# A two-layer transformer kernel on one core: first-stage loads laid out by tile, constant matmuls, token tiles in pairs

## The chip, the core and the metric

The kernel runs on one core of a Trainium2 chip. A core has five engines with queues of their own: PE (TensorE: matmuls and transposes through the array), DVE (VectorE), ACT (ScalarE), POOL (GpSimd) and SP (SyncE, which here issues nearly all DMAs). Results of PE go to PSUM, which has eight banks; everything else lies in SBUF or in HBM. The metric is the device time of one execution in microseconds, and the median of several executions is compared.

## The reference, cut to what matters

Two layers run over 1024 tokens of width 1024, with 256 context tokens beside them. Layer 0 is attention with 16 query heads and 4 key/value heads; layer 1 is neighbourhood attention. Each layer starts with a norm that is modulated by a conditioning vector, and ends with a gated output projection.

```
silu_c = jax.nn.silu(c); silu_cc = jax.nn.silu(c_ctx)
for i in range(DEPTH):
    mod_x = (silu_c @ w_mod[i] + b_mod[i])[:, None, :]
    mod_c = silu_cc @ w_mod[i] + b_mod[i]
    sh_x, sc_x, g_x = jnp.split(mod_x, 3, axis=-1)
    sh_c, sc_c, g_c = jnp.split(mod_c, 3, axis=-1)
    hx = rms_norm(x, norm_g[i]) * (1.0 + sc_x) + sh_x
    hc = rms_norm(ctx, norm_g[i]) * (1.0 + sc_c) + sh_c
    if i % N_MIXERS == 0:
        yx, yc = gqa_axial_mixer(hx, hc, a_w_in[ia], ..., a_w_out[ia], cos, sin, not last)
    else:
        yx, yc = neighbourhood_mixer(hx, hc, b_w_in[ib], b_rpb[ib], b_w_out[ib], not last)
    x = x + g_x * yx
    if not last:
        ctx = ctx + g_c * yc
return rms_norm(x, final_norm_g)

# gqa_axial_mixer, its beginning
px = hx @ w_in                      # columns: q 1024, k 256, v 256, z 1024
q = apply_axial_rope(rms_norm(q, q_g), cos, sin)
k = apply_axial_rope(rms_norm(k, k_g), cos, sin)
pkv = hc @ w_in[:, A_WIDTH:A_WIDTH + 2 * A_KV_WIDTH]
```

## The kernel before

Tokens are cut into ten tiles of 128: tiles 0 to 7 are x, tiles 8 and 9 the context. The width of 1024 is cut into eight steps, kt = 0 to 7. Matmuls that need more than f16 are done three times, with both factors split into a high and a low f16 part (hi·hi, hi·lo, lo·hi).

**First stage.** For each kt, `mod_cols` loads two f32 tiles `wm` (512 KiB each, in two DMAs of 256 KiB whose contiguous pieces are 512 B) of the layer's modulation weights. It multiplies them with the conditioning vector (`pm`), copies the row (`mrow`), turns it into columns (`pmc`) and forms the scale and shift, `acol` and `scol`. The pool has seven `wm` buffers, so the loads can run three and a half steps ahead. `ln_pre` loads a token tile (`xstage`, 512 KiB) and normalises it in place. `h_kt(t0, n, kt)` transposes one kt block of n token tiles on PE (`pl`), applies scale and shift on ACT (`tf`), and splits into a high part (a cast) and a low part (a subtract), both on DVE. `load_w` loads 256 KiB of weights (`wskv`), scales them to a high part on ACT and takes the low part on DVE. `kv_mm` does three matmuls of 512 columns per tile and kt into the tile's k/v bank (`pkv`). `kv_post` takes v out, normalises and rotates k (`norm_rope_split`: `sq`, `qss`, a power on POOL `qrs`, `t1k`, `t2k`, a multiply with `qrs`, the split `q16k`) and transposes it (`pkt`).

The first part of the stage is the loop over kt for tiles 0 to 3, which keeps four banks open. The second part transposes tiles 4 to 7, four at a time, and the context tiles, and runs tiles 4 to 9 through two banks at a time. Then layer 0's attention follows: per pair of heads a projection (`pa`, with weights `wsa`), scores, softmax and values, on all engines. Output projection (`poa`), layer 1's projections (`pb`, `pvz`, weights `wsb`), its attention (`bsn`, `bpv`) and the last projection (`pob`, weights `wsob`) end the program.

**What sets the order.** The code is written out once in a rough order (the functions `timeline` and `items` give each piece of work a place). Then `Planner` builds a graph of all instructions with a table of costs, lists them for each engine, goes back from the end to due times, and lists them again five times; the best list becomes the order on each engine. So each change in code or costs may move instructions anywhere.

What the changed lines call is below, with the profile's line numbers.

Of the kernel before, what the change touches and what calls it, by code (L numbers as in the profile page):

```python
# [40 lines left out]
PFB, PHB, PTB = 5, 5, 8  # L41


class Planner:
# [42 lines left out]
    def cost(self, x, rd, wr):  # L87
# [6 lines left out]
        if e == "PE":  # L94
            f32 = ins[0].dtype == mybir.dt.float32
            cols = self.elems(outs[0])
            passes = (2 if x.is_transpose else 4) if f32 else 1
# [59 lines left out]
    def graph(self):  # L157
# [60 lines left out]
        for i, x in enumerate(self.node):  # L218
# [4 lines left out]
            before[e] = i  # L223

# [33 lines left out]
    def schedule(self, key=None, margin=0.0, scale=None):  # L258
# [62 lines left out]
        while count < N:  # L321
# [86 lines left out]
            for j in succ[i]:  # L408
                rdy[j] = max(rdy[j], fin + self.SEM[self.eng[j]] + margin if self.eng[j] != e or e != "PE" else 0.0)
# [6 lines left out]
    def deadlines(self, margin):  # L416
# [14 lines left out]
        for i in sorted(range(N), key=lambda i: -start[i]):  # L431
            e, d = self.eng[i], done[i] - start[i]
            for j in self.succ[i]:
                due[i] = min(due[i], due[j] - (0.0 if self.eng[j] == e == "PE" else d + self.SEM[self.eng[j]] + margin))
# [47 lines left out]
def trunk_kernel(ctx, tc, x, cx, cc, norm_g, ng_row, b_cols, sel_c, w_mod, b_mod, a_w_in, a_qg, a_kg, a_w_out,  # L482
                 b_w_in, rpb, b_w_out, fin_g, cos_t, sin_t, mask_q, out):
# [29 lines left out]

    cct = main.tile([P, 2 * KT], F32, name="cct")
# [186 lines left out]
    def norm_rope_split(pool, sqs, psv, alt, nt, nh, t0, gc, gs, gplain, nm):  # L701
# [26 lines left out]
        if alt is None:  # L728
            V.tensor_tensor(t1, t1, rb, op=ALU.mult)
# [17 lines left out]

    def a_src(kt0, nk, ncol):

        starts = ncol  # L750
        wd = 512 // (nk * len(starts))
        step = starts[1] - starts[0] if len(starts) > 1 else wd

        def f(st):
            for j in range(nk):
                a = a_w_in[(kt0 + j) * P:(kt0 + j + 1) * P, starts[0]:starts[0] + 1]
                src = bass.AP(a.tensor, a.offset, [[2560, P], [step, len(starts)], [1, wd]])
                ins = DM.dma_start(st[:, j * (512 // nk):(j + 1) * (512 // nk)].rearrange("p (r c) -> p r c", c=wd),
                                   src)
            return ins  # L760
        return f
# [27 lines left out]
    def h_kt(t0, n, kt):  # L789
# [8 lines left out]
        V.tensor_copy(hi[:, kt, c], tv)  # L798
# [20 lines left out]
    def ps_kv(t):  # L819
        tag = "st" if t % 4 < 2 else "pv"  # L820
# [6 lines left out]
    for kt in range(KT):  # L827
        load_w(wkv, a_src(kt, 1, [1024, 1280]), kt, 1, 512, f"kv{kt}")
        if kt + 1 < KT:
            mod_cols(kt + 1, wmp)  # L830
        if kt >= 4:
            ln_pre(kt)
# [3 lines left out]
        for t in range(4):  # L836
            kv_mm(banks[t], t, kt)
    for t in range(8, 10):
# [358 lines left out]
    def load_wout(src, nm):  # L1197
        ws = []
        wout[nm] = ws
        for hf in range(2):  # L1200
# [325 lines left out]
    items.append((load_wout(b_w_out, "b"), 6.9, 7.2, 1600))  # L1526
# [112 lines left out]
```

## Time and profile before

| what | value |
|---|---|
| three runs | 1380.61, 1385.62, 3514.45 us; median 1385.62 |
| the profiled execution | 1390.31 us, its span 1388.5 us |
| PE busy | 1331.3 us, 96% of the span |
| DVE, ACT, POOL busy | 73%, 66%, 46% |
| DMA | 198.22 MB, 143 GB/s on average, the queues 65% busy |
| first k/v matmul of tiles 0 to 3 | 23.7 us |
| first matmul of tiles 4 to 9's part (after the last of tiles 0 to 3) | 64.2 us |
| first projection of layer 0's queries (`pa`) | 108.6 us |

The page's busy times are for one execution. A line of the chain or of the waits names an engine, a line of the kernel and the tile. A wait is put down to what came last. In the views by stretch the busy time of each engine stands with its number of instructions, and the granted clock is that of PE.

### The profile page before, as it was taken

The page shows a single profiled execution, that of the slowest core. Times are in us where ns is not written, and L with a number is a line of the kernel's source. Part 1 is how long each engine was busy: PE and PEld are TensorE (multiplying, and loading weights), DVE is VectorE, ACT ScalarE, POOL GpSimd, SP SyncE. Part 2 cuts the span into 40 slices and gives each one's busy share as a digit, 9 for nine tenths or more (in the row PEclk, how much of TensorE's full clock was granted, in tenths as well). Part 3 has the DMA queues.
Part 4 walks back from the last instruction along what each step waited for, and adds up shares of the span by engine and source line. Part 5 has one row for each costly group of instructions (what it writes and reads, how often), then busy time and mean ns, then how long its engine had stood idle before and what let it go on. Part 6 is the DMA issues. An engine that isn't in the chain of part 4 may idle for free.

```text
span 1388.5 us, 34562 instructions
## 1 busy us (share of the span) xinstructions
PE 1331.3 (96%) x13082; PEld 921.5 (66%) x13082; DVE 1008.4 (73%) x2674; ACT 911.8 (66%) x2178; POOL 641.3 (46%) x811
## 2 busy tenths in 40 slices
PE   5799999999999999999999999999999999999897
PEld 3457777777767677676554476867767686867543
DVE  3597887879878888889347746677776768687733
ACT  2553687878787787687733427677777767787811
POOL 2222677777677768677954301212122222322332
PEclk9999999999999999999999999999999999999999
DMA  9744458778688878674328734576766756587922
GB/s 266 241 118 114 89 122 161 141 154 171 125 162 158 159 149 162 130 194 122 112 86 214 185 91 114 103 150 126 128 136 119 150 106 150 94 173 136 215 84 99
DMA packets 478927, 198.22 MB, mean 143 GB/s; under 512 B 383328, under 2 KB 455968, under 8 KB 478760
## 3 DMA queue, kind: packets, MB, share of 16 engines
q1 hardware_dynamic: 478184, 195.99, 65.2%
q8 instruction: 102, 1.67, 0.5%
q14 instruction: 65, 0.53, 0.1%
q10 hardware_dynamic: 576, 0.03, 0.0%
HBM read 90.51 MB, written 15.22 MB: 76 GB/s over the span
## 4 chain that ended last, share of the span: by engine, by line
PE 71%; DVE 12%; DMA 6%; ACT 5%; issue 3%; POOL 2%; SPq 0%; DVEq 0%; POOLq 0%; ACTq 0%
PE pvz L1378 11%; PE pa L928 11%; PE pb L1345 9%; PE poa L1258 7%; PE pob L1550 5%; PE pkv L803 3%; PE st L1165 2%; PE st L1166 2%; DVE mxp L959 2%; PE bpv L1458 2%; PE pm L958 2%; DMA qpt<-qpp 2%; DMA xstage<-in_x 2%; PE qpv L1086 1%; PE pv L1034 1%
## 5 line engine op out<-in xcount | busy, mean ns | idle before, releaser
L1027 POOL TENSOR_TENSOR pl<-pf,ph 128x256 f16<-128x256 f32 x340 | 234.4, 715 | 58.7 <-ACT pf L1152 43.0
L1027 POOL TENSOR_TENSOR bph<-bpf,bph 128x256 f16<-128x256 f32 (+1 forms) x128 | 98.2, 778 | 312.7 <-ACT bpf L1449 248.0
L928 PE MATMUL pa<-wa,x 128*128 128x256 f16 x1536 | 212.4, 272 | 0.0
L1345 PE MATMUL pb<-hb_hi,wb 128*128 128x512 f16 (+1 forms) x640 | 192.6, 358 | 0.5 <-DVE bk L1364 0.4
L1378 PE MATMUL pvz<-wb,hb_hi 128*128 128x256 f16 x1024 | 176.2, 273 | 3.7 <-DVE bk L1364 3.2
L1150 ACT ACTIVATE ph<-st 128x512 f16<-128x512 f32 x200 | 119.1, 604 | 69.3 <-PE st L1166 56.5
L928 PEld LDWEIGHTS <-x 128*128 128x128 f16 x1536 | 143.0, 97 | 32.2 <-issue 1.1
L1345 PEld LDWEIGHTS <-wb 128*128 128x128 f16 x960 | 92.6, 98 | 73.7 <-issue 1.5
L1378 PE MATMUL pvz<-wb,hb_lo 128*128 128x256 f16 x512 | 139.6, 273 | 0.0
L959 DVE TENSOR_REDUCE mxp<-pm 128x1 f32<-128x512 f32 x160 | 107.8, 683 | 20.5 <-PE pm L958 19.6
L1152 ACT ACTIVATE pf<-st 128x512 f32<-128x512 f32 x200 | 118.7, 608 | 1.8 <-POOL pl L1027 1.8
L1378 PEld LDWEIGHTS <-hb_hi 128*128 128x128 f16 x1024 | 97.1, 98 | 26.9 <-DVE bk L1364 5.8
L1345 PE MATMUL pb<-hb_lo,wb 128*128 128x512 f16 (+1 forms) x320 | 114.5, 358 | 0.0
L1027 POOL TENSOR_TENSOR qpp<-qpf,qpp 128x512 f16<-128x512 f32 x84 | 97.3, 1178 | 35.9 <-ACT qpf L1109 31.0
L1033 PE MATMUL pv<-v,ph 128*128 128x65 f16 x800 | 105.5, 193 | 0.2 <-DVE og L1015 0.2
L1034 PE MATMUL pv<-v,ph 128*128 128x64 f16 x800 | 105.0, 195 | 0.0
L1035 PE MATMUL pv<-v,pl 128*128 128x65 f16 x800 | 102.7, 192 | 1.7 <-DVE pl L1024 1.4
L1447 ACT ACTIVATE bph<-bpf,bnx 128x384 f16<-128x384 f32 (+1 forms) x128 | 69.7, 584 | 36.8 <-DVE bnx L1439 36.5
L1429 DVE CUSTOM_DVE_ANT_0 bpf<-bsn,tb 128x384 f32<-128x384 f32 x96 | 53.0, 552 | 55.5 <-PE bsn L1410 53.4
L1550 PE MATMUL pob<-wob,ob 128*128 128x512 f16 x384 | 87.3, 379 | 3.3 <-DVE bmx L1429 1.1
L1033 PEld LDWEIGHTS <-ph 128*128 128x128 f16 x800 | 75.8, 97 | 20.9 <-DVE og L1015 0.4
L1035 PEld LDWEIGHTS <-pl 128*128 128x128 f16 x800 | 76.1, 99 | 14.4 <-POOL pl L1027 3.5
(268 smaller groups left out, 3802.5 us busy)
## 6 DMA issues: line engine op xcount, KB each, us to landing
wg<-in_w_mod SPq DMA_DIRECT2D x64, 256.0 KB
wsb<-in_b_w_in SPq DMA_DIRECT2D x64, 256.0 KB
wm<-in_w_mod SPq DMA_DIRECT2D x32, 256.0 KB
wsa<-in_a_w_in SPq DMA_DIRECT2D x64, 128.0 KB
xstage<-in_x SPq DMA_DIRECT2D x8, 512.0 KB
wsoa<-in_a_w_out SPq DMA_DIRECT2D x16, 256.0 KB
x<-in_x SPq DMA_DIRECT2D x8, 512.0 KB
x_d<-x SPq DMA_DIRECT2D x8, 512.0 KB
```

The source lines that it names most:

```text
L928: T.matmul(ps[:, :, i, :], hA(a, kt, t), wt[w][:, kt, :], start=n == 0, stop=n == 3 * KT - 1)
L959: V.tensor_reduce(mxs[i][:, t, ch:ch + 1], pm, axis=AX.X, op=ALU.max)
L1027: G.tensor_tensor(lo[:, c], p32[:, c], hi[:, c], op=ALU.subtract)
L1033: T.matmul(pv[:, t, :], hi[:, c], v[:, 0:65], start=first and t == 0, stop=False)
L1034: T.matmul(pv[:, t, 0:HD], hi[:, c], v[:, 65:129], start=False, stop=False)
L1035: T.matmul(pv[:, t, :], lo[:, c], v[:, 0:65], start=False, stop=last and t == n - 1)
L1150: S.activation(ph, st, AF.Exp)
L1152: S.activation(p32, st, AF.Exp)
L1258: T.matmul(ps, lhs(a, kt), w[b][:, kt, :], start=n == 0, stop=n == 3 * KT - 1)
L1345: T.matmul(ps[:, 0:n].rearrange("p (t q) -> p t q", q=P), wt[a][:, kt, which * P:(which + 1) * P], hb[b][:, c0 // P:(c0 + n) // P, kt], st ...
L1378: T.matmul(ps[:, :, j, :], hb[a][:, t, kt], wt[w][:, kt, 256:512], start=m == 0, stop=m == 3 * KT - 1)
L1550: T.matmul(ps, ob[kt][:, t // 4, a, c], wout["b"][hf][b][:, kt, :], start=n == 0, stop=n == 3 * KT - 1)
```

## The change

Layouts on the host: the modulation weights of layer 0 become `w_mod0`, in which one `wm` tile is one piece of 4 KiB per partition, loaded by one DMA of 512 KiB. The k/v columns are a tensor of their own (`a_kv`). The q/z columns of a pair (`a_qz`) and layer 1's input weights (`b_in`) lie so that each load reads pieces of 2 KiB and not of 512 B.

In the program: 101 matmuls of a constant tile (`warm`, 256 columns) that depend on nothing else and whose result nobody reads. A soft rule for the planner (`BEHIND`): the loads of x tiles 4 to 7 are issued after that of `wskv7`. Tiles 4 to 7 are transposed in two pairs, not four at a time. For all tiles but 0 to 3 the cast to the high part moves from DVE to POOL, and for k tiles the multiply with `qrs` and the subtract of the split move from DVE to POOL. Half 0 of the last projection's weights gets an earlier place in the rough order.

```
+BEHIND = [(f"xstage{t}", "wskv7") for t in range(4, 8)]
...
+        for late, early in BEHIND:
+            self.soft.add((writer[early], writer[late]))
+            self.pred[writer[late]].add(writer[early])
...
+    wone = main.tile([P, 2 * P], F16, name="wone")
+    V.memset(wone, 1.0)
+    warm = ps_mx("warm")
+    def warm_up(n):
+        for _ in range(n):
+            T.matmul(warm[:, 0:2 * P], wone[:, 0:P], wone, start=True, stop=True)
+    warm_up(1)
...
-            for r in range(2):
-                a = w_mod[0, 4 * j * P:4 * j * P + P, r * D + kt * P:r * D + kt * P + 1]
-                DM.dma_start(wm[:, :, r, :], bass.AP(a.tensor, a.offset, [[3 * D, P], [P * 3 * D, 4], [1, P]]))
+            DM.dma_start(wm.rearrange("p a b c -> p (a b c)"), w_mod0[kt, j])
...
-        if alt is None:
-            V.tensor_tensor(t1, t1, rb, op=ALU.mult)
+        off = alt is None
+        if off:
+            G.tensor_tensor(t1, t1, rb, op=ALU.mult)
...
-        V.tensor_tensor(q16[:, :, 1, :], alt, q16[:, :, 0, :], op=ALU.subtract)
+        (G if off else V).tensor_tensor(q16[:, :, 1, :], alt, q16[:, :, 0, :], op=ALU.subtract)
...
-        V.tensor_copy(hi[:, kt, c], tv)
+        (G if t0 else V).tensor_copy(hi[:, kt, c], tv)
...
-        load_w(wkv, a_src(kt, 1, [1024, 1280]), kt, 1, 512, f"kv{kt}")
+        load_w(wkv, lambda st, kt=kt: DM.dma_start(st, a_kv[kt]), kt, 1, 512, f"kv{kt}")
...
-        if kt >= 4:
-            ln_pre(kt)
+        if kt >= 6:
+            ln_pre(2 * kt - 8)
+            ln_pre(2 * kt - 7)
...
+    warm_up(100)
...
-        h_kt(4, 4, kt)
+        h_kt(4, 2, kt)
         if kt % 2:
             kv_post(banks[kt // 2], kt // 2)
+    for kt in range(KT):
+        h_kt(6, 2, kt)
...
-            load_w(wa[u], a_src(2 * j, 2, [u * P, 1536 + u * P]), 2 * j, 2, 256, f"a{u}{j}")
+            load_w(wa[u], lambda st, j=j: DM.dma_start(st, a_qz[u, :, 512 * j:512 * j + 512]), 2 * j, 2, 256, f"a{u}{j}")
...
-                a = b_w_in[kt * P:(kt + 1) * P, u * P:u * P + 1]
-                DM.dma_start(st.rearrange("p (r c) -> p r c", c=P),
-                             bass.AP(a.tensor, a.offset, [[4 * D, P], [D, 4], [1, P]]))
+                DM.dma_start(st, b_in[u, :, kt * 512:kt * 512 + 512])
...
-    items.append((load_wout(b_w_out, "b"), 6.9, 7.2, 1600))
+    items.append((load_wout(b_w_out, "b", (0,)), 6.05, 6.9, 800))
+    items.append((load_wout(b_w_out, "b", (1,)), 7.0, 7.3, 800))
```

**How the order moves.** Three places, with the numbers of the tiles; the last figure of a name only tells buffers apart.

SP at the very start, before: `wm00` and `wm01` are the two halves of step 0's modulation weights, each loaded by two DMAs, `xstage0` is x tile 0.

```order
L551 DMA wm00_149<-in_w_mod 128x4x128
L551 DMA wm01_152<-in_w_mod 128x4x128
L781 DMA xstage0_107<-in_x 128x1024
L551 DMA wm10_215<-in_w_mod 128x4x128
L551 DMA wm11_218<-in_w_mod 128x4x128
L781 DMA xstage1_108<-in_x 128x1024
L781 DMA xstage2_109<-in_x 128x1024
```

The second DMAs of these four, `xstage3`, and the first DMAs of steps 2 and 3 follow before `wskv0`, the first k/v weights: twelve `wm` DMAs and four x tiles in all. SP at the same place now:

```order
L795 DMA xstage0_111<-in_x 128x1024
L795 DMA xstage1_112<-in_x 128x1024
L795 DMA xstage2_113<-in_x 128x1024
L795 DMA xstage3_114<-in_x 128x1024
L579 DMA wm00_153<-in_w_mod0 128x1024
L579 DMA wm01_155<-in_w_mod0 128x1024
L579 DMA wm10_217<-in_w_mod0 128x1024
L579 DMA wm11_219<-in_w_mod0 128x1024
L842 DMA wskv0_213<-in_a_kv 128x512
```

The four x tiles are issued first, then steps 0 and 1 of `wm`, each in two DMAs and not in four, and `wskv0`.

SP in the later half of the first part, before: x tiles 4 to 7 among the k/v weights of steps 4 to 7.

```order
L781 DMA xstage4_111<-in_x 128x1024
L758 DMA wskv4_399<-in_a_w_in 128x512
L781 DMA xstage5_112<-in_x 128x1024
L551 DMA wm60_459<-in_w_mod 128x4x128
L551 DMA wm61_462<-in_w_mod 128x4x128
L781 DMA xstage6_113<-in_x 128x1024
L758 DMA wskv5_455<-in_a_w_in 128x512
```

And now, from `wskv4` on:

```order
L842 DMA wskv4_393<-in_a_kv 128x512
L579 DMA wm60_442<-in_w_mod0 128x1024
L579 DMA wm61_444<-in_w_mod0 128x1024
L579 DMA wm70_487<-in_w_mod0 128x1024
L579 DMA wm71_489<-in_w_mod0 128x1024
L842 DMA wskv5_438<-in_a_kv 128x512
L842 DMA wskv6_483<-in_a_kv 128x512
L842 DMA wskv7_555<-in_a_kv 128x512
L795 DMA xstage4_115<-in_x 128x1024
L795 DMA xstage5_116<-in_x 128x1024
L781 DMA ct_151<-in_cos_t 128x512
```

The x tiles stand behind all weights of the first part; `ct` (a rope table), `gk`, `sn`, tiles 6 and 7 and the context tiles follow.

POOL at the beginning of the second part, before: the four rope tables and two norms, then only the powers of the k tiles (`qrsk`).

```order
L774 TENSOR_TENSOR gck_139<-ct_147,gk_132 128x512
L775 TENSOR_TENSOR gsk_140<-sn_148,gk_132 128x512
L609 TENSOR_TENSOR rs_ln_617<-ms_ln_615,mhalf_75 128x1
L609 TENSOR_TENSOR rs_ln_627<-ms_ln_625,mhalf_75 128x1
L774 TENSOR_TENSOR gcq_129<-ct_147,gq_131 128x512
L775 TENSOR_TENSOR gsq_130<-sn_148,gq_131 128x512
L711 TENSOR_TENSOR qrsk0_657<-qssk0_655,mhalf_75 128x4
```

And now, from the first cast (`x10` is the high part of x tiles 4 to 7, `tf40` the scaled block of kt 0 of the pair 4, 5):

```order
L812 CAST x10_109<-tf40_725 128x256
L812 CAST x10_109<-tf41_732 128x256
L739 TENSOR_TENSOR qrsk0_741<-qssk0_739,mhalf_75 128x4
L812 CAST x10_109<-tf42_763 128x256
L758 TENSOR_TENSOR t1k0_743<-t1k0_743,qrsk0_741 128x256
L812 CAST x10_109<-tf43_770 128x256
L739 TENSOR_TENSOR qrsk1_779<-qssk1_777,mhalf_75 128x4
L762 TENSOR_TENSOR q16k0_749<-t1k0_743,q16k0_749 128x4x64
```

Casts, powers, multiplies and splits alternate on POOL; 24 casts stand there up to the last that a k/v matmul of the context needs, with eight powers and fifteen multiplies and subtracts among them, and the tables `gcq` and `gsq`.

On PE the 101 constant matmuls stand ahead of the first `pkv`: 70 at the very start, then 11, 8, 4 and 8 between the first transposes and the first `pm` and `pmc`; the second `pm`, a step of transposes and the second `pmc` come after them, ahead of the first `pkv`. The eight loads of half 0 of `wsob` stand between the same transposes of layer 1 as before.

More of the change, by code (lines that the diff above doesn't have):

```diff
@@ L96, in cost @@
             cols = self.elems(outs[0])
+            if outs[0].bass_ap.tensor.name.startswith("warm"):
+                return 130.0, 170.0
             passes = (2 if x.is_transpose else 4) if f32 else 1
@@ L223, in graph @@
             before[e] = i
+        self.soft = set()
+        writer = {}
+        for i, x in enumerate(self.node):
+            if type(x).__name__ == "InstDMACopy" and x.outs and hasattr(x.outs[0], "bass_ap"):
+                writer.setdefault(x.outs[0].bass_ap.tensor.name.rsplit("_", 1)[0], i)
+        for late, early in BEHIND:
+            self.soft.add((writer[early], writer[late]))
+            self.pred[writer[late]].add(writer[early])
         self.glued = set()
@@ L481, in trunk_kernel @@
 @with_exitstack
-def trunk_kernel(ctx, tc, x, cx, cc, norm_g, ng_row, b_cols, sel_c, w_mod, b_mod, a_w_in, a_qg, a_kg, a_w_out,
-                 b_w_in, rpb, b_w_out, fin_g, cos_t, sin_t, mask_q, out):
+def trunk_kernel(ctx, tc, x, cx, cc, norm_g, ng_row, b_cols, sel_c, w_mod, w_mod0, b_mod, a_qz, a_kv, a_qg, a_kg, a_w_out,
+                 b_in, rpb, b_w_out, fin_g, cos_t, sin_t, mask_q, out):
     nc = tc.nc
@@ L746, in trunk_kernel @@
     sqk = sq_tiles(lp)
[L748 to L761, printed above, removed]
     ct = lp.tile([P, NX, HD], F32, name="ct")
@@ L1195, in trunk_kernel, with load_wout @@
     wout = {}
[L1197 to L1200, printed above, removed]
+    def load_wout(src, nm, halves=(0, 1)):
+        ws = wout.setdefault(nm, [])
+        for hf in halves:
             w = x_pair(hf, f"wo{nm}{hf}")
@@ L1600 @@
     rp = np.pad(i["b_rpb"][0].transpose(0, 2, 1), ((0, 0), (0, 0), (8, 8)))
+    aw = i["a_w_in"][0]
     arrs = {
@@ L1614 @@
         "a_w_out": i["a_w_out"][0],
-        "b_w_in": i["b_w_in"][0],
+        "b_in": i["b_w_in"][0].reshape(KT, P, 4, KT, P).transpose(3, 1, 0, 2, 4).reshape(KT, P, 4 * D),
         "rpb": rp,
```

15 lines of the change are left out of this document (12 added, 3 removed).

## The prediction

> **What bounds the kernel now.** I read the page first, then busy time by stretch, cut where PE changes its work, then the list of PE's waits, then the order of time in the first 110 us. Span 1388.5 us; the profiled execution took 1390.31 us, and the median of the three runs shown is 1385.62 us. The page's part 1:
>
> ```profile
> PE 1331.3 (96%) x13082; PEld 921.5 (66%) x13082; DVE 1008.4 (73%) x2674; ACT 911.8 (66%) x2178; POOL 641.3 (46%) x811
> ```
>
> PE is idle for only 57 us, so the question is where those are. Busy time by stretch (after the limits and the length come busy us and count of PE, PEld, DVE, ACT, POOL, then granted clock, DMA share, GB/s):
>
> ```profile
> core 0: us, PE busy (x) PEld busy (x) DVE busy (x) ACT busy (x) POOL busy (x), PEclk, DMA share, GB/s
> 0.00:23.70 23.70, 10.03 (x56) 5.76 (x57) 7.74 (x25) 8.17 (x13) 7.76 (x15) 1.00 0.98 279
> 23.70:64.20 40.50, 37.00 (x241) 17.91 (x239) 20.43 (x51) 15.26 (x26) 4.90 (x8) 0.96 0.82 254
> 64.20:108.60 44.40, 40.24 (x218) 21.62 (x217) 41.28 (x106) 24.41 (x56) 15.23 (x14) 0.92 0.51 121
> 108.60:240.00 131.40, 128.23 (x1460) 101.45 (x1458) 107.36 (x284) 87.89 (x187) 80.90 (x103) 1.00 0.58 124
> 240.00:660.00 420.00, 406.10 (x5169) 304.62 (x5168) 352.74 (x949) 327.97 (x671) 306.28 (x387) 0.99 0.74 152
> ...
> 1200.00:1310.00 110.00, 104.57 (x998) 74.81 (x997) 87.68 (x259) 89.39 (x270) 34.64 (x45) 1.00 0.84 160
> ```
>
> The first stage is the first three rows: 23.7 us up to the first k/v matmul, 40.5 us in which the eight kt steps of tiles 0 to 3 run (the "first part"), 44.4 us for tiles 4 to 9 (the "second part"). PE idles 13.7 + 3.5 + 4.2 = 21.4 us there, and in parts of it runs at a lower clock. From 108.6 to 660 us it idles 3.2 + 13.9 = 17.1 us in 551, and 5.4 us in the stretch near the end. Who PE waits for:
>
> ```profile
> PE pl L793 <- DVE xstage L786: 10.9, 2, 10.8
> PE qpv L1086 <- DMA qpt<-qpp: 5.4, 7, 1.1
> PE pkv L803 <- DVE t2k L720: 3.2, 1, 3.2
> PE pkv L803 <- ACT wkv L642: 1.3, 1, 1.3
> ```
>
> Three of these four are in the first stage; qpv is the attention's.
>
> **The first part.** Order of time on PE, one kt step whole and two broken ones:
>
> ```profile
> 23.71 4.34 PE L803 MATMUL pkv<-wkv,x 128*128 128x512 f16 x12
> 33.97 2.76 PE L803 MATMUL pkv<-wkv,x 128*128 128x512 f16 x12
> 36.57 0.50 PE L560 MATMUL pmc<-sel,mrow 128*128 128x2 f32 x4
> 37.00 1.07 PE L555 MATMUL pm<-wm,s 128*32 128x256 f32 x16
> 42.52 0.60 PE L793 MATMUL pl<-idf,xstage 128*128 128x128 f32 x4
> 43.05 1.07 PE L555 MATMUL pm<-wm,s 128*32 128x256 f32 x16
> 46.55 4.44 PE L803 MATMUL pkv<-wkv,x 128*128 128x512 f16 x12 [1.28 <-ACT wkv L642]
> ```
>
> The twelve matmuls from 33.97 take 2.60 us from start to next start, 0.217 each. The same twelve take 4.34 and 4.44 us at 23.71 and 46.55, when PE had been idle before: about 1.7 us lost each time. The next rows are SP's and ACT's; the number after the start is the length.
>
> ```profile
> 38.67 0.50 SPq L781 DMA_DIRECT2D xstage<-in_x  x1
> 39.27 0.38 SPq L758 DMA_DIRECT2D wskv<-in_a_w_in  x1
> 45.89 0.61 ACT L642 ACTIVATE wkv<-wskv 128x512 f16<-128x512 f32 x1
> 22.64 0.62 ACT L642 ACTIVATE wkv<-wskv 128x512 f16<-128x512 f32 x1
> ```
>
> wskv4 was issued at 39.27 and used at 45.89. It lies among x tiles 4 to 7, which this part does not need; that wait is what PE stood for at 46.55.
>
> *Start.* In the SP order, 5.25 MiB are issued up to and including wskv0 before (twelve wm pieces of 0.25, four x tiles of 0.5, 0.25), and 4.25 MiB now (four x tiles, four wm of 0.5, 0.25). Scaling 22.64 us gives 18.3 us. ACT's 0.62 us follows, and PE has the second pm and pmc ahead of the first pkv; I take 20.5 us for the first pkv against 23.7. Bounds: 18.9 us (18.3 and the 0.62) and 23.7 (no gain). The 101 warm matmuls stand on PE before that, 70 of them ahead of any transpose. At 0.217 x 256/512 = 0.11 us, or twice that before the clock comes up, they take 11 to 22 us. At the lower figure they fit into the 13.7 us in which PE idles; if the clock came up only after all of them, the last transposes of x would start some 3 us late. I cost them at nothing and keep 3 us.
>
> *The eight steps.* One step at full clock: 2.60 + 0.43 (pmc, 36.57 to 37.00) + 1.07 (pm) + 0.53 (pl, 42.52 to 43.05) = 4.6 us, eight of them 37. Already done before the first pkv are three pl, two pm, two pmc: 4.6 us. So 32.4 us of PE work, and 33.5 us with 1.1 us of stalls, because the warm start takes away 1.7 us, the wskv wait goes, and with it the second slow spell. Before: 40.5. Loads do not set it: up to wskv7 it is 12 MiB, 12.6 MB, which even at 279 GB/s is issued and moved by 45 us, while the last step starts near 51. The wm buffers hold three and a half steps, as before. First part ends at 54.0 instead of 64.2. Bounds 52 and 61 (all of the 1.7 us spells stay).
>
> **The second part.** In the new order x tiles 4 and 5 follow wskv7: 13 MiB, 13.6 MB, which at 279 GB/s are there by 49 us, 5 us ahead of their use; the tables come right behind (51 us), so t2k, for which PE waited 3.2 us, is no longer late, and tiles 6 and 7 by 54 us, 13 us ahead. PE has 144 pkv at 0.217 = 31.2, 44 transposes at 0.53/4 = 5.8, and 40 transposes of k with 128 columns, by columns 0.054 each = 2.2: 39.2 us. What is new here is POOL's load:
>
> ```profile
> L798 DVE CAST x<-tf 128x512 f16<-128x512 f32 x8 | 4.1, 511 | 0.0
> L799 DVE TENSOR_TENSOR x<-tf,x 128x512 f16<-128x512 f32 x8 | 6.2, 772 | 0.0
> L798 DVE CAST xc_hi<-tf 128x256 f16<-128x256 f32 x8 | 2.3, 283 | 0.0
> L799 DVE TENSOR_TENSOR xc_lo<-tf,xc_hi 128x256 f16<-128x256 f32 x8 | 3.3, 413 | 0.0
> L729 DVE TENSOR_TENSOR t1k<-t1k,qrsk 128x256 f32<-128x256 f32 x9 | 3.7, 413 | 0.0
> L711 POOL TENSOR_TENSOR qrsk<-qssk,mhalf 128x4 f32<-128x4 f32 x9 | 10.8, 1205 | 27.0 <-DVE qssk L709 27.0
> L1027 POOL TENSOR_TENSOR pl<-pf,ph 128x256 f16<-128x256 f32 x340 | 234.4, 715 | 58.7 <-ACT pf L1152 43.0
> ```
>
> DVE loses 4.1 + 2.3 us of casts and, for nine k tiles, a multiply and a subtract of that size, 0.41 each, 7.4; its eight subtracts of 0.772 become sixteen of 0.413, +0.4. 41.3 becomes 27.9 us. POOL gets 24 casts (16 pair-steps and 8 of ctx) and 20 two-input operations. No row shows a cast on POOL: its bounds are 0.283 (DVE's, same size) and 0.715 (POOL, same size, two inputs); I take 0.5, the middle. Up to the last cast, which PE needs, POOL does 24 x 0.5 + 15 x 0.715 + 8 powers x 1.2 + 2.9 for two tables (rows below) = 35.2 us. That is under PE's 39.2, but near it, and the two engines get in each other's way:
>
> ```profile
> 65.75 1.45 POOL L774 TENSOR_TENSOR gcq<-ct,gq 128x512 f32<-128x512 f32 x1
> 66.31 1.18 DVE L798 CAST x<-tf 128x512 f16<-128x512 f32 x1
> 67.16 1.46 POOL L775 TENSOR_TENSOR gsq<-sn,gq 128x512 f32<-128x512 f32 x1
> 67.75 1.43 DVE L799 TENSOR_TENSOR x<-tf,x 128x512 f16<-128x512 f32 x1
> 69.10 0.41 DVE L798 CAST x<-tf 128x512 f16<-128x512 f32 x1
> 69.77 0.68 DVE L799 TENSOR_TENSOR x<-tf,x 128x512 f16<-128x512 f32 x1
> ```
>
> Beside a POOL operation the cast took 1.18 instead of 0.41 us and the subtract 1.43 instead of 0.68: each ended just after POOL did. With 44 more POOL operations, if a third meet a DVE instruction of this kind at 0.3 to 0.75 us, DVE gets 5 to 11 us back: 33 to 39 us. Three engines at 35 to 39 us, in a chain: I put 42.4 us, 3.2 over PE's work. Bounds 39.2 and the 44.4 of before; beyond that the first rival. The Trainium skill ("SBUF — State Buffer", Who interferes with whom) calls this an exclusive lock that DVE's copies, casts and two-input operations share with POOL, and so speaks against moving such work to POOL. The two stretched rows agree. By the rule taken to its end, all DVE time added to POOL's without the powers, 27.9 + 25.6 = 53.5 us would stand for 42.4, and 11.1 us of the gain would go.
>
> The second part then ends at 54.0 + 42.4 = 96.4 us: 12.2 us earlier than 108.6.
>
> **The other edits.** After 108.6 us PE is the bound and its work is the same, so the shift passes on. The weights of the pairs (wsa, wsb) are now read in 2 KiB rows and not in 512 B pieces. Two stretches of 4 us, the first nearly all wm in 512 B pieces, the second x, ct and ctx in longer rows:
>
> ```profile
> 16.00:20.00 4.00, 3.87 (x29) 1.80 (x22) 1.65 (x6) 0.66 (x2) 0.55 (x1) 1.00 1.15 298
> 52.00:56.00 4.00, 3.44 (x34) 1.76 (x30) 2.65 (x8) 2.20 (x4) 0.86 (x1) 1.00 1.02 382
> ```
>
> 7 MiB of wsa at 298 and at 382 GB/s are 24.6 and 19.2 us of transfer, 5 us less over 550 us, so about 1 us of the 5.4 us for which PE waits on qpt. I put -1, with 0 and -5 as bounds. wsb gains nothing: it has 16 pieces per pair under a PE that works. The Trainium skill ("DMA: Bandwidth & Descriptors", Specifications) puts the line rate at pieces of 512 B and more, by which the layout gains no rate and this -1 becomes 0; the two rows differ by 28%, in loads that differ in more than their piece size. Half 0 of the last weights, which the diff moves, stands at the same place in SP's order; it is costed at nothing. The rest of the program is ordered anew, and the order in the attention differs widely; with 13.9 us of idle time in 240 to 660, I give that 6 us either way and 0 as the likeliest.
>
> **The sum.** -3.2 - 7.0 - 2.0 - 1.0 = -13.2 us: a span of 1375.3, 1377.1 us for an execution like the profiled one, and from the median shown, 1385.62, to **1372 us**.
>
> **The rivals.**
> *POOL sets the second part; slower.* The place is POOL's row of casts, in order with the k work. If it begins at 52 us, tables, powers and two short ones take 12.5 us and 39 casts and two-input operations m each; the last cast comes after 108.6 us if m is over 1.13 us. At 1.46, POOL's length for 512 columns, it ends at 121.4: 12.8 us slower, less 1: 1397 us. For it: the stretched rows. Against: 340 POOL operations of this size, beside a busy DVE, take 0.715. Chance 0.10.
> *The gain is given back in the attention.* The new order there costs 6 to 10 us: 1378 to 1382. For it: the idle time is 17 us, each us of it from another cause; against: PE, DVE, ACT and POOL have the same work. 0.16.
> *The change does less than it says.* The clock is still slow at the first pkv and the steps stall as before: only the start and the second part, -6: 1380. 0.12.
> *More.* Second part at 39.2, first at 32.4, and 6 us in the attention: -23.5: 1362 us. 0.14.
> The forecast itself has 0.48, within 1366 to 1379.
>
> The range, 1359 to 1385, takes in the second, third and fourth and leaves out the first and the tails. A difference of 2%, 27.7 us, is about what a measurement of this kernel can tell from no change. Faster than 1357.9 needs everything of the fourth case and 4 us more: 0.08. Slower than 1413.3 would need POOL at twice its price: 0.02. Within: 0.90.
>
> **What would show it.** In the profile after: the first pkv near 20.5 us and twelve of them in 2.7 us from the start; ACT's wkv less than 4 us behind its issue for wskv4; the first part's end near 54, pa starting near 96; POOL's casts near 0.5 us, and pkv waiting for x by POOL by less than 4 us in all; PE idle from there to 660 us near 17 us. Wrong would be: casts over 1 us, twelve slow pkv at the start, or an attention whose idle time grew by what the first stage gained.

## The result, and the profile after

The changed kernel takes 1365.72 us in the median against 1385.36 us for the kernel before in the same comparison: a ratio of 0.9865 with a 95% interval of 0.9831 to 0.9899. That is 1.0 to 1.7% faster, clear of noise and within 2%. The forecast was 1372 us, with a range of 1359 to 1385. One run of each kernel was disturbed and counts in neither ratio.

The profiled execution of the changed kernel took 1365.58 us, close to its median. That of the kernel before took 1390.31, some 5 us over its own. The two spans, 1363.8 and 1388.5 us, therefore differ by 24.7 us where the medians differ by 19.6. The sums below are of profiles.

Part 1 of the page after:

```profile
PE 1329.9 (98%) x13183; PEld 927.6 (68%) x13183; DVE 1003.1 (74%) x2647; ACT 910.2 (67%) x2186; POOL 664.7 (49%) x855
```

Busy time by stretch, cut at the first pkv, at the end of the eighth kt step, at the first pa, at the first poa (the attention's output projection) and at the first pb:

```profile
core 0: us, PE busy (x) PEld busy (x) DVE busy (x) ACT busy (x) POOL busy (x), PEclk, DMA share, GB/s
0.00:18.53 18.53, 17.33 (x154) 13.70 (x154) 10.65 (x23) 7.39 (x12) 7.71 (x15) 1.00 0.92 340
18.53:51.40 32.87, 32.68 (x240) 16.72 (x240) 20.24 (x50) 14.00 (x24) 3.63 (x6) 1.00 0.91 341
51.40:94.90 43.50, 39.81 (x224) 20.76 (x223) 40.63 (x87) 30.48 (x69) 37.13 (x56) 1.00 0.49 125
94.90:627.00 532.10, 522.90 (x6542) 400.58 (x6541) 443.29 (x1216) 405.97 (x841) 382.60 (x486) 1.00 0.73 147
627.00:766.00 139.00, 135.72 (x1035) 70.36 (x1032) 80.66 (x130) 66.30 (x125) 81.23 (x94) 1.00 0.55 146
```

The same view of the kernel before, from its first pa to its first poa, the stretch that answers to the fourth of these rows:

```profile
108.60:651.40 542.80, 525.73 (x6543) 401.36 (x6541) 451.95 (x1219) 409.24 (x844) 380.50 (x481) 0.99 0.71 145
```

So the start is 5.2 us shorter (18.5 for 23.7), the first part 7.6 (32.9 for 40.5), the second part 0.9 (43.5 for 44.4), and the stretch to the first poa 10.7. Together that is 24.4 of the 24.7 us. PE idled for 17.1 us in that last stretch before (542.80 less 525.73), and for 9.2 now.

Of the waits that the prediction spoke of, these are left in the changed kernel (us in total, times, longest); that for qpt was 5.4 us before:

```profile
PE pkv L817 <- DVE t2k L748: 1.3, 1, 1.3
...
PE qpv L1104 <- DMA qpt<-qpp: 0.6, 1, 0.6
...
PE pkv L817 <- POOL x L812: 0.5, 1, 0.5
```

### The profile page after: what moved, and what is told of

Read it like the earlier page. It is cut to its first block, busy times and chain, and to the rows that moved or that the text cites. A ratio compares the mean times of both kernels' runs of the same rounds, so it can differ in the third digit from the quotient of the medians.

```text
span 1363.8 us, 34709 instructions
## 1 busy us (share of the span) xinstructions
PE 1329.9 (98%) x13183; PEld 927.6 (68%) x13183; DVE 1003.1 (74%) x2647; ACT 910.2 (67%) x2186; POOL 664.7 (49%) x855
## 4 chain that ended last, share of the span: by engine, by line
PE 68%; DVE 11%; ACT 9%; DMA 5%; POOL 3%; issue 3%; SPq 1%; DVEq 0%; POOLq 0%; ACTq 0%
PE pa L946 11%; PE pb L1360 9%; PE pvz L1393 9%; PE poa L1275 7%; PE pob L1566 6%; PE st L1183 2%; PE st L1184 2%; PE pkv L817 2%; ACT bpf L1464 2%; PE pm L976 2%; PE bpv L1473 1%; PE pv L1052 1%; PE qpv L1104 1%; PE pv L1053 1%; PE pv L1051 1%
## 5 line engine op out<-in xcount | busy, mean ns | idle before, releaser
L977 DVE TENSOR_REDUCE mxp<-pm 128x1 f32<-128x512 f32 x160 | 107.9, 684 | 13.7 <-PE pm L976 12.3
L1051 PEld LDWEIGHTS <-ph 128*128 128x128 f16 x800 | 75.8, 97 | 19.0 <-ACT ph L1168 0.7
L1052 PEld LDWEIGHTS <-ph 128*128 128x128 f16 x800 | 75.5, 97 | 12.6
```

Source lines behind the costliest of these rows:

```text
L977: V.tensor_reduce(mxs[i][:, t, ch:ch + 1], pm, axis=AX.X, op=ALU.max)
L1051: T.matmul(pv[:, t, :], hi[:, c], v[:, 0:65], start=first and t == 0, stop=False)
L1052: T.matmul(pv[:, t, 0:HD], hi[:, c], v[:, 65:129], start=False, stop=False)
```

## The clock in both profiles

In these traces PE's granted clock falls to one half for stretches of 3.41 us or a multiple of that. All of them start on a grid of that length, whose place against the program differs from profile to profile. Cutting the trace on that grid shows what goes before one. Six windows of the kernel before, four of the first stage and two of the attention (the column behind POOL's is the granted clock):

```profile
44.00:47.41 3.41, 1.59 (x12) 0.93 (x9) 1.86 (x6) 2.58 (x5) 0.55 (x1) 1.00 1.05 349
47.41:50.82 3.41, 3.41 (x9) 1.25 (x8) 2.33 (x5) 1.67 (x3) 0.55 (x1) 0.50 1.10 345
...
67.89:71.30 3.41, 1.40 (x4) 0.65 (x4) 3.41 (x7) 3.20 (x6) 2.16 (x2) 0.50 0.57 95
71.30:74.72 3.42, 3.42 (x13) 2.03 (x12) 3.42 (x9) 1.37 (x3) 0.32 (x1) 0.50 0.53 49
...
450.16:453.57 3.41, 1.61 (x18) 0.92 (x15) 2.11 (x6) 2.74 (x6) 2.85 (x5) 1.00 0.25 49
453.57:456.98 3.41, 3.41 (x10) 1.09 (x8) 3.01 (x8) 2.72 (x7) 3.14 (x5) 0.50 0.99 184
```

A window in which PE was busy for 47% of the time, in pieces, is followed by one at half the clock, in which a PE that is busy throughout loses 1.7 us. The profile of the kernel before has 17.1 us of such stretches ahead of its end, at 47.4, 67.9 (twice the length), 453.6 and 559.4 us. PE was busy for 15.0 us of them: all through, but for the first half of the one at 67.9, in which it was busy for 1.40 us. The changed kernel's profile has none. Its nearest case in the first stage is this one, at 53%:

```profile
52.80:56.21 3.41, 1.81 (x10) 0.97 (x10) 3.36 (x9) 2.98 (x8) 1.72 (x5) 1.00 0.46 42
56.21:59.62 3.41, 3.22 (x18) 1.50 (x16) 3.41 (x8) 3.16 (x8) 3.41 (x5) 1.00 0.40 36
```

Half of 15.0 is 7.5 us, so just under a third of the profiles' difference is clock and not work or waits: 4.1 us of it in the first stage, 3.4 in the attention. The twelve slow `pkv` at 23.71 us in the kernel before, ahead of the clock's first rise, come on top, with 1.6 us (4.34 against 2.75). Other runs agree: seven runs of the kernel before that were timed beside the first experiments had a mean granted clock of 0.991 to 0.997, and three of the changed kernel 0.999.

The Trainium skill ("TensorE: Matmul & The Clock Gate", What's actually happening) has the free-running window of this length, and has the clock fall after an idle one. The traces agree on the window; the condition that they show is weaker, since the window ahead was half busy.

## The experiments

The changed kernel gained more than forecast, and most of the excess lay in the attention. The open questions were which edits paid in the first stage, and why the attention gained 10.7 us where the forecast had 1. All ratios below are to the kernel before, timed beside each run; the profiles are one of each kernel. In most runs the planner draws the order anew. Two runs with the same line numbers and the same order on every engine as the changed kernel differ from it in their transfers alone; they are named as such.

**Without the constant matmuls.**

```
-    warm_up(1)
-    warm_up(100)
```

> The changed kernel without its 101 constant matmuls. Theory (the clock is what they buy): PE stands idle until the first transposes near 10.7 us, the first twelve pkv take 4.3 us in place of 2.75, what stands ahead of them runs at half rate too, and the first part ends 2 to 3 us later: 1368 to 1370 us against 1365.7. Rival (the transposes and modulation matmuls of 10 to 18 us bring the clock up by themselves): first pkv in 2.8 us, total within 1 us of 1365.7. Second rival (the matmuls stand in the way of the first transposes): first pkv earlier than 18.5 us and 1363 to 1365.

Measured: 1369.88 us, ratio 0.9892 (0.9866 to 0.9917). PE in order of time:

```profile
8.70 0.66 PE L800 MATMUL pl<-idf,xstage 128*128 128x128 f32 x2 [8.70 <-DVE xstage L793]
...
18.48 1.49 PE L810 MATMUL pkv<-wkv,x 128*128 128x512 f16 x3
19.76 0.85 PE L581 MATMUL pmc<-sel,mrow 128*128 128x2 f32 x4
20.48 2.37 PE L810 MATMUL pkv<-wkv,x 128*128 128x512 f16 x9
```

And of the changed kernel:

```profile
1.20 9.65 PE L541 MATMUL warm<-wone 128*128 128x256 f16 x70 [1.20 <-DVE twos L572]
10.69 0.38 PE L807 MATMUL pl<-idf,xstage 128*128 128x128 f32 x2
...
18.53 2.75 PE L817 MATMUL pkv<-wkv,x 128*128 128x512 f16 x12
```

The first pkv comes at the same time with and without them, so they are hidden, as costed. Without them everything up to 20.5 us runs at half rate: two transposes take 0.66 in place of 0.38 us. The first pa comes at 98.5 in place of 94.9 us, 1.7 of it for a half-clock stretch at 58.6; as this order too is a new draw, that stretch can't be put down to the missing matmuls alone. The total is 4 us longer. The intervals of the two ratios overlap, the single runs (1368.1 to 1371.3 against 1363.9 to 1365.9) don't. The theory's 1368 to 1370 holds.

**All of the second part's work on DVE.**

```
-        (G if t0 else V).tensor_copy(hi[:, kt, c], tv)
+        V.tensor_copy(hi[:, kt, c], tv)
-            G.tensor_tensor(t1, t1, rb, op=ALU.mult)
+            V.tensor_tensor(t1, t1, rb, op=ALU.mult)
-        (G if off else V).tensor_tensor(q16[:, :, 1, :], alt, q16[:, :, 0, :], op=ALU.subtract)
+        V.tensor_tensor(q16[:, :, 1, :], alt, q16[:, :, 0, :], op=ALU.subtract)
```

> The changed kernel with the casts of tiles 4 to 9 and the k tiles' multiply and subtract back on DVE. Theory (POOL carries 25 us of work that DVE hadn't the time for): DVE is busy for nearly all of the second part again, which takes 45 us in place of 43.5; 1367 to 1368. Rival (the two engines get in each other's way, so that moving work gains nothing): DVE's subtracts go back from 0.705 to 0.41 us, the second part takes 43.5 us or less; 1364 to 1366.

Measured: 1364.9 us, 0.9854 (0.9829 to 0.9879), not told apart from the changed kernel. Its second part, and its subtract of the pairs there:

```profile
52.00:95.50 43.50, 39.72 (x221) 20.67 (x220) 40.91 (x122) 28.78 (x65) 15.51 (x15) 1.00 0.40 98
```

```profile
L813 DVE TENSOR_TENSOR x<-tf,x 128x256 f16<-128x256 f32 x16 | 6.7, 416 | 0.0
```

And in the changed kernel, DVE's subtract and POOL's casts:

```profile
L813 DVE TENSOR_TENSOR x<-tf,x 128x256 f16<-128x256 f32 x16 | 11.1, 705 | 1.5 <-POOL x L812 1.5
...
L812 POOL CAST x<-tf 128x256 f16<-128x256 f32 x16 | 9.1, 577 | 0.0
```

POOL is busy for 37.13 us in one and 15.51 in the other, DVE for 40.63 and 40.91, and the stretch takes 43.50 us in both. What was moved off DVE are casts of 5.3 and 2.3 us and a multiply and a subtract of 3.3 each, 14.2 us by their durations. Of that, 5.5 us came back, since the subtracts that stayed take 0.705 in place of 0.416 us for the pairs and 0.546 in place of 0.416 for ctx; another 3.4 us went into four more pieces of wa (1.4 us for two, 4.8 for six), work for the attention that DVE did within the part. The rival holds for the total: moving this work gained nothing. The subtracts did go back as it said, and the theory's 45 us for the part didn't come. Since DVE was as busy in both runs, they don't show what the part would take if DVE were really less busy. What they show is that PE was busy for 39.8 and 39.7 of the 43.5 us, and that its longest wait there was of one kind in both, for t2k by DVE, 1.3 and 1.6 us.

**Tiles 4 to 7 four at a time.**

```
-        h_kt(4, 2, kt)
+        h_kt(4, 4, kt)
...
-    for kt in range(KT):
-        h_kt(6, 2, kt)
```

> The changed kernel with tiles 4 to 7 done four at a time again (eight casts and eight subtracts of 512 columns in place of sixteen of 256). Theory (pairs are worth little, since the x tiles are there by then): second part within 1 us of 43.5, 1365 to 1367. Rival (pairs let PE begin tiles 4 and 5 while 6 and 7 are not normalised): PE idles 3 us more between 50 and 60 us, 1368 to 1370. The order in the attention is drawn anew here, which the trace must separate.

Measured: 1369.45 us, 0.9894 (0.9865 to 0.9923). PE's waits in its first stage have one that the changed kernel lacks, and the window in which it lies is followed by half the clock:

```profile
PE pl L807 <- DVE xstage L800: 2.7, 2, 1.8
```

```profile
52.80:56.21 3.41, 0.90 (x6) 0.42 (x6) 3.30 (x7) 2.81 (x7) 2.44 (x3) 1.00 0.22 19
56.21:59.62 3.41, 3.27 (x12) 1.63 (x12) 3.24 (x10) 3.27 (x8) 3.34 (x5) 0.50 0.24 73
```

That is the rival: with pairs, PE has tiles 4 and 5 to work on while 6 and 7 are being normalised. The first pa is 1.9 us later (96.8); the other 2 us of the 3.7 lie behind it, in an order drawn anew with a half-clock stretch at 465.8 us, and can't be put down to the pairs.

**Without the rule on x tiles 4 to 7.**

```
-BEHIND = [(f"xstage{t}", "wskv7") for t in range(4, 8)]
+BEHIND = []
```

> The changed kernel without the rule that x tiles 4 to 7 are issued behind the last k/v weights (wskv7); the order after the first stage is nearly the changed kernel's. Theory (the forecast's: the wait for wskv4 of 1.3 us and the slow spell of 1.7 us behind it come back): first pa 2 to 3 us later, 97 to 98 us, total 1367 to 1369. Rival (with 4 KiB rows the loads are far enough ahead in either order): first pa within 1 us of 94.9, total 1365 to 1366.5.

Measured: 1365.2 us, 0.9852 (0.9827 to 0.9878). With the new layouts the planner by itself puts only two x tiles ahead of wskv7. On PE the theory's wait and slow spell are back, if smaller:

```profile
44.62 4.52 PE L817 MATMUL pkv<-wkv,x 128*128 128x512 f16 x12 [0.79 <-ACT wkv L670]
```

Its granted clock is at one half from 45.6 to 49.0 us. The first pa comes at 96.3, which is later than the rival's limit (95.9) and sooner than the theory's 97 to 98. In the total nothing of it is seen, and there the rival holds.

**The first stage's weights in short pieces, in the same order.** The planner is given the old prices for these loads, so that the order stays.

```
-            DM.dma_start(wm.rearrange("p a b c -> p (a b c)"), w_mod0[kt, j])
+            DM.dma_start(wm.rearrange("p a b c -> p (a b) c"), w_mod0[kt, j, :, :, 0:P])
-        load_w(wkv, lambda st, kt=kt: DM.dma_start(st, a_kv[kt]), kt, 1, 512, f"kv{kt}")
+        load_w(wkv, lambda st, kt=kt: DM.dma_start(st.rearrange("p (r c) -> p r c", c=2 * P), a_kv[kt, :, :, 0:2 * P]), kt, 1, 512, f"kv{kt}")
```

> The changed kernel in its own order on every engine, but with the modulation weights read in 512 B pieces and the k/v weights in 1 KiB pieces, as before the change. Theory (the order of the loads brings the start forward, as the forecast had it): first pkv by 19.5 us, 1366 to 1367. Rival (the pieces set the rate): 4.46 MB up to the first k/v weights at 298 GB/s in place of 400 take 15.0 us in place of 11.2, first pkv near 22 us, a step's 1.31 MB takes 4.4 us against 4.6 us of PE, so nothing is caught up: 1369 to 1370.

Measured: 1364.85 us, 0.9857 (0.9838 to 0.9877). Eight us of loading in this kernel, and then in the changed kernel (last column, GB/s):

```profile
8.00:12.00 4.00, 4.00 (x39) 3.61 (x38) 2.38 (x6) 1.90 (x4) 1.05 (x3) 1.00 1.19 299
12.00:16.00 4.00, 4.00 (x46) 3.00 (x43) 1.43 (x4) 0.00 (x0) 0.13 (x1) 1.00 1.20 298
```

```profile
8.00:12.00 4.00, 4.00 (x40) 3.60 (x37) 2.15 (x7) 2.05 (x4) 1.10 (x2) 1.00 1.02 380
12.00:16.00 4.00, 4.00 (x45) 3.02 (x43) 1.81 (x6) 0.40 (x1) 0.55 (x1) 1.00 1.03 412
```

The same bytes in the same order move at 298 GB/s in the short pieces (512 B for wm, 1 KiB for k/v) and at about 400 in the rows (4 and 2 KiB). In this run the short pieces also lie apart in the source, with a gap of a piece's length behind each, which was not varied by itself. The first pkv comes at 20.5 in place of 18.5 us, the first pa at 97.3 in place of 94.9. So the layout is 2 of the 5.2 us that the start gained; the other 3 go with the order of the loads, and with half as many DMAs for wm, which this run keeps. Neither theory's total was met: by the first pb the 2.4 us had gone (766.2 against 766.0 us), in stretches where PE idled a little less, and the totals cannot be told apart.

**Another draw of the order.**

```
-        plan.refine(5, 100.0, 300.0)
+        plan.refine(5, 100.0, 310.0)
```

> The changed kernel with one number of the planner's deadlines at 310 in place of 300 ns: the same instructions in another order, above all in the attention. Theory (the order in the attention is a draw, worth some us either way): first pa within 2 us of 94.9, the stretch from there to the first poa 531 to 537 us, PE idle there 9 to 13 us; total 1364 to 1371. Rival (the change's own order is an exceptional draw): 540 us or more, idle near 17 us.

Measured: 1368.66 us, 0.9889 (0.9866 to 0.9912); from the first pa to the first poa 534.1 us with PE idle for 11.1. The theory holds for the attention, though the first pa came at 98.7 and not within 2 us of 94.9: this draw has a wait and a half-clock stretch in the second part.

The same line changed in the kernel before:

> The kernel before with the same number of its planner at 310: another draw of the order with the old layouts. Theory (a draw): the stretch from the first pa to the first poa falls into the range that the changed kernels show, 531 to 537 us against 542.8 before, total 1374 to 1383. Rival (the old layouts hold the attention back in whatever order): 540 us or more, qpt waits of 4 us or more, total 1383 to 1388.

Measured: 1382.44 us, 0.998 (0.9957 to 1.0003). The first pa came at 104.2 us, 4.4 us sooner than before, and the median is 3.6 us under the 1386.01 of the kernel before beside it, so the attention was no faster. For the attention the rival holds; the total is one that the theory had. Its stretch from first pa to first poa, in a profiled run of 1391.4 us, 9 us over the median, with 10.2 us at half clock in that stretch:

```profile
104.20:650.00 545.80, 528.26 (x6554) 402.68 (x6551) 450.36 (x1220) 410.01 (x846) 380.01 (x483) 0.99 0.70 143
```

**The kernel before with only the layout of the q and z weights.**

```
-        load_w(wa[u], a_src(2 * j, 2, [u * P, 1536 + u * P]), 2 * j, 2, 256, f"a{u}{j}")
+        load_w(wa[u], lambda st, j=j: DM.dma_start(st, a_qz[u, :, 512 * j:512 * j + 512]), 2 * j, 2, 256, f"a{u}{j}")
```

> The kernel before with only the q and z weights laid out by pair, one DMA of 2 KiB rows for two of 1 KiB in 512 B pieces. Theory (worth a microsecond, the rest is a draw): first stage as before (pa near 108.6), then 531 to 543 us, depending on the draw. Rival (this layout is the attention's whole gain): the stretch from the first pa to the first poa is 533 us or less, qpt waits under 1 us, total 1374 to 1376.

Measured: 1378.51 us, 0.9955 (0.9939 to 0.9971), faster than the kernel before by 7.5 us in the medians and 6.2 by the ratio. The first pa came at 108.0 us, and then:

```profile
108.00:637.50 529.50, 519.96 (x6529) 399.56 (x6528) 446.11 (x1218) 405.99 (x842) 375.13 (x481) 1.00 0.72 148
```

The stretch is the rival's, though its total (1374 to 1376) and its waits for qpt (under 1 us; PE's matmuls waited 2.5) did not come. In this draw, the one edit gives the whole gain of the attention. What is left, from 0.9955 to the changed kernel's 0.9865, is 0.9% or 12.5 us, and the forecast had 12.2 for the first stage.

**What it is about that layout.** The edit does three things at once: pieces of 2 KiB for 512 B, one DMA for two, and with both a lower price in the planner, which then orders the attention differently. The first run keeps the changed kernel's order and has short pieces; the second has short pieces and lets the planner know; the third has whole rows in two DMAs of 1 KiB.

```
-            load_w(wa[u], lambda st, j=j: DM.dma_start(st, a_qz[u, :, 512 * j:512 * j + 512]), 2 * j, ...
+            load_w(wa[u], lambda st, j=j: DM.dma_start(st.rearrange("p (r c) -> p r c", c=P), a_qz[u, :, 4 * j:4 * j + 4, 0:P]), 2 * j, ...
```

> The changed kernel in its own order on every engine, but with the q and z weights (wsa) read in 512 B pieces as before. Theory A (the attention gained 10 us from another order, not from the layout): the same waits as in the changed kernel, 1365 to 1367, PE idle from 95 to 640 us near 9 us. Theory B (the layout is what freed the queue; PE's waits for qpt fell from 5.4 to 0.6 us by it): waits for qpt come back to 3 us or more, 1370 to 1376. My forecast had 1 us for this layout: 1367.

> The changed kernel with the q and z weights in 512 B pieces, one DMA per load, and a planner that counts them at the higher price (1.06 in place of 0.80 us each), so that it orders the attention for it. Theory N (the number of DMAs on SP is what counts): as in the run with these pieces in the changed order, instructions waiting for qpt 8 us or less in all, first pa to first poa 530 to 537 us. Theory P (the plan drawn up under the cheaper price is what counts): 12 us or more of waits for qpt, 540 us or more.

```
+            load_w(wa[u], lambda st, j=j: [DM.dma_start(st[:, 256 * h:256 * h + 256], a_qz[u, :, 512 * j + 256 * h:512 * j + 256 * h + 256]) for h in range(2)][1], 2 * j, ...
```

> The changed kernel with each load of q and z weights in two DMAs of 1 KiB rows, as many DMAs as before the change but whole rows. Theory N (the number): 12 us or more of waits for qpt, first pa to first poa 540 us or more, total 1372 or more. Theory P (the price): 8 us or less, 530 to 537 us, total 1364 to 1369.

Measured: 1367.25 us (0.9871, 0.9844 to 0.9899), 1364.68 (0.985, 0.9826 to 0.9875) and 1363.66 (0.9844, 0.9816 to 0.9873). First pa to first poa in the three:

```profile
96.10:630.70 534.60, 524.41 (x6542) 401.27 (x6541) 442.06 (x1216) 406.99 (x841) 382.66 (x486) 1.00 0.74 146
```

```profile
97.80:626.90 529.10, 520.74 (x6528) 400.22 (x6527) 438.14 (x1212) 406.27 (x841) 383.30 (x485) 1.00 0.73 146
```

```profile
94.60:626.10 531.50, 521.57 (x6543) 400.55 (x6542) 444.64 (x1215) 407.48 (x844) 382.22 (x487) 1.00 0.73 148
```

The time that PE's matmuls and weight loads together stood waiting for qpt (us, times) in the view of that tile, first in the kernel before and in its other draw:

```profile
  DMA qpt<-qpp: 13.9, 16
```

```profile
  DMA qpt<-qpp: 16.7, 13
```

and in the kernel before with the new layout, then in the changed kernel:

```profile
  DMA qpt<-qpp: 6.8, 8
```

```profile
  DMA qpt<-qpp: 3.2, 8
```

In the three variants it is 5.9, 3.5 and 5.3 us. So neither the pieces, nor the pieces with their price, nor the number of DMAs brings the old waits back by itself. Short pieces in the unchanged order cost 2.7 us of these waits and 1.5 us in the medians, which its interval does not tell from nothing. What stays open is which combination does it: two DMAs, each of 512 B pieces and each priced so, with rows 10 KiB apart in the source, were not tried in the changed kernel. That it is the old layout and not a lucky draw rests on two orders with it (PE idle for 17.1 and 17.5 us in the stretch) against twelve profiles of ten orders without it, the changed kernel and all experiments but one (8.4 to 12.4 us); two of the twelve had short pieces, in one DMA. The waits for qpt alone part the two groups less clearly: they are 2.8 to 10.7 us in the twelve.

**An attempt at a better version.** All of the second part on DVE, and the post work of the finished tiles first:

```
-        h_kt(4, 2, kt)
-        if kt % 2:
-            kv_post(banks[kt // 2], kt // 2)
+        if kt < 4:
+            kv_post(banks[kt], kt)
+        h_kt(4, 2, kt)
```

> An attempt at a better version: the changed kernel with all of the second part's work on DVE again, and the four finished k tiles' post work ahead of the transposes of tiles 4 and 5 in the program, so that the banks for tiles 4 and 5 come free earlier. If PE's waits at 50 to 60 us (t2k 1.6, tf 0.9, x 1.0 us with all on DVE) are a matter of that order, 2 to 3 us go and first pa comes at 92 to 93 us: 1361 to 1363. If DVE is simply full there, the waits move to the transposes and it is 1364 to 1366.

Measured: 1369.17 us, 0.9882 (0.9856 to 0.9909). The waits moved to the transposes and grew, and the gaps brought the clock down for 10.2 us in the second part:

```profile
PE pl L807 <- ACT tf L809: 4.2, 4, 2.8
```

The first pa came at 101.7 us. No version was found that is clearly faster than the changed kernel; the one with two DMAs of 1 KiB has the lowest median, 2 us less, with an interval that overlaps.

## Why the prediction was right, and where it wasn't

**The start: -3.2 forecast, -5.2 measured.** The bytes ahead of the first k/v weights were counted rightly; the rate was not. I scaled by bytes alone, and the new rows also move faster. The run with short pieces in the same order has ACT's first wkv at 18.28 us and its first pkv at 20.5 us, the forecast's 18.3 and 20.5. The constant matmuls cost nothing, as put: 70 of them took 9.65 us, where the two rates of the prediction give 7.7 and 15.

**The first part: -7.0 forecast, -7.6 measured.** It ended at 51.4 in place of the forecast's 54.0 us, because it began sooner. The slow first pkv were gone (2.75 us for twelve), and so was the second slow spell. The cause that I gave for that spell, a wait for weights behind the x tiles, is borne out in the profile: without the rule on these tiles a wait of 0.8 us and twelve pkv of 4.52 us came back. Its worth is not, since the total is the same. One sign that I named was wrong. wskv4 was to be used less than 4 us behind its issue; it was used over 7 us behind, the second of the two here, and PE had other work until then:

```profile
22.33 0.38 SPq L842 DMA_DIRECT2D wskv<-in_a_kv  x1
```

```profile
29.41 1.14 ACT L670 ACTIVATE wkv<-wskv 128x512 f16<-128x512 f32 x2
```

**The second part: -2.0 forecast, -0.9 measured, for another reason.** POOL's casts took 0.577 and 0.494 us for the 0.5 assumed, DVE was busy for 40.6 us and not 33 to 39. The mechanism was wrong, though: the step took DVE's relief for a gain, DVE's time filled up again, and the run with all on DVE has the same 43.5 us. What this part did lose is time at half clock, worth 2.4 us before (half of 1.40 and 3.42), which is more than the 0.9 gained. From the first pkv to the first pa the two parts went from 84.9 to 76.4 us. PE's idle time there fell from 7.7 to 3.9 us, the stretches at half clock, worth 4.1, are gone, and so are the slow first pkv, worth 1.6. These three make 9.5 us, one more than the 8.5 gained; 464 matmuls lie there now for 459. The first rival's price, 1.13 us per operation, was never near. The lock rule that was weighed against the sum would have given 53.5 us for the part and was too strong; the stretched subtracts show that the contention is there.

**The attention: -1 forecast, -10.7 in the profiles.** This is the term that failed, in its size. By the medians it is less, about 6 us: 19.6 less the 13.7 of the first stage. I priced the layout by transfer time, 5 us over 550, of which a fifth counted. The run with short pieces in the changed order fits that price. But the kernel before with this layout alone is 7.5 us faster (4.0 to 8.5 by its interval). Of the 7.9 us of idle time that went in the profiles, 4.8 are the matmuls' waits for qpt (5.4 to 0.6). Most of what else went is clock, 3.4 us, and the longest waits in the windows ahead of the two half-clock stretches were not for qpt:

```profile
452.66 0.59 PE L1166 MATMUL st<-q,k 65*128 65x512 f16 x2 [1.80 <-DMA q<-zt]
559.07 0.27 PE L1098 MATMUL qs<-k,q 128*128 128x256 f16 x1 [1.55 <-DVE qmx L1101]
```

I gave the new order 6 us either way as a draw. The stretch took 542.8 and 545.8 us in the two orders with the old layout and 529 to 537 in the ten without it, so it was one-sided. The sign of 17 us of idle time up to 660 us was wrong with it: it is 12.5.

**Rivals and range.** The range of 1359 to 1385 holds the result; the likeliest case's own, 1366 to 1379, misses it by 0.3 us. The case "more", at 1362, is nearer than 1372. It had 6 us in the attention, which is where the excess was, but also a second part of 39.2 us, which didn't come. The total came out 6.3 us from the forecast while the second part came for another reason and the attention was out by 5 to 10 us; that the result lies in the range all the same is in part luck. I had the slow spell behind a wait in the first part's sum, but not in the other terms, where a wait of 1.8 us can cost up to 3.5 as well.

## What to carry to other kernels

Price a gap on TensorE with what follows it: here a 3.41 us window with PE busy for less than 46% was followed by one at half the clock, which cost up to another 1.7 us, so closing many small gaps gained more than their own length. When a layout changes what a planner believes of its loads, measure the layout in an unchanged order and the order apart; here the first was worth 1.5 us in the medians, not told from nothing, and both together 6 to 7.5. Work taken from DVE and put on POOL does not spare DVE its full length: here over a third of it came back as longer instructions, other work filled much of the rest, and the stage took 43.5 us either way.

## What the runs showed of the hardware

In the fourteen profiles of this case, outside the first 20 and the last 10 us, every window of that grid in which PE was busy for less than 46% is followed by one at half the clock. Of the windows at full clock that were busy for more than 62%, none is; between the two it went both ways. An example for no fall, in the changed kernel at 47%:

```profile
646.70:650.11 3.41, 1.59 (x28) 1.03 (x27) 0.00 (x0) 0.38 (x1) 2.03 (x4) 1.00 0.59 169
650.11:653.52 3.41, 2.25 (x24) 1.25 (x24) 1.04 (x3) 2.16 (x5) 0.65 (x2) 1.00 0.00 0
```

Since the grid is not tied to the program, the same gap falls into one window in one run and is split in the next. That could explain why the kernel before varies by 10 us from run to run (1380.6 to 1390.3), but only in part. Of 28 further runs of it, the four with a mean granted clock of 0.996 or more took 1382.2 to 1382.9 us, while the four at 0.995 lie anywhere from 1380.9 to 1388.2.

The granted clock reads 1.00 from the first microsecond on in every profile, although in the run without constant matmuls everything up to 20.5 us ran at half rate. The traces' first entry of that clock begins later: at 21.0 us in that run, at 5.0 in the changed kernel and at 26.9 in the kernel before, which is where the matmuls come up to full rate in each. The 1.00 ahead of it is the lack of an entry and not a reading. In the changed kernel the constant matmuls start 0.213 us apart up to 5.0 us and 0.109 apart from there on, 3.8 us after the first.

Loads in rows of 4 and 2 KiB moved a third faster than in pieces of 512 B and 1 KiB that lay apart in the source, the same bytes in the same order (about 400 against 298 GB/s). The Trainium skill ("DMA: Bandwidth & Descriptors", Specifications) puts full rate at 512 B and more. Here the loads in the smaller pieces, none under 512 B, stayed a quarter below the others, and the measurement decides; what part the gaps between the pieces have in it is not shown.
